# A fused decoder layer: half a weight unit copied by VectorE, gate projections copied out by ScalarE, query transposes moved

## The chip, the cores and the metric

The kernel runs on one core of one Trainium2 chip (1 of 8). The metric is the device time of one execution in microseconds (us). The core has TensorE (PE in the rows, its weight loads PEld), VectorE (DVE), ScalarE (ACT), GpSimd (POOL) and SyncE (SP, which issues the transfers). Each takes its own instructions in order.

## What is computed

One decoder layer over 512 tokens of width 1024, in float32. In the reference's words, cut:

```python
h = rmsnorm(x, g_mix)
x_rnn, g_rnn, q, k, v, gate_a, gate_b = split(h @ w_in)
y_a = (rg_lru(causal_conv(x_rnn)) * gelu(g_rnn)) @ w_rnn_proj
y_b = sliding_window_attention(q, k, v) @ w_attn_proj     # 16 query heads, 4 key heads, window 128
x = x + (sigmoid(gate_a) * y_a + sigmoid(gate_b) * y_b) @ w_out
x = x + square(relu(rmsnorm(x) @ w_up)) @ w_down
x = x + (p @ w_ple_proj) * sigmoid(rmsnorm(x) @ w_ple_gate)
```

Attention normalises queries and keys by head, rotates them, and each token sees itself and the 127 tokens ahead of it; every head has a sink value in its softmax.

## The kernel before

Activations lie transposed, features on the 128 partitions and the 512 tokens along the row. Every large product is made of three products of fp32r (a rounded float32 that TensorE takes at its full rate): a value is split into a high part, rounded to fp32r, and a low part, the rest; high x high, high x low and low x high are added up in PSUM (`mm3`, L144 to L147).

The weights come as 143 units of 128 x 1024 values. `wissue` takes the next unit of a fixed list and calls `wsplit` (L109): SyncE issues the transfer into `wr` (2 buffers), ScalarE writes the high part `wh` (L118), VectorE the low part `wl` (L119). Three further units are kept ready ahead of the one in use (`AHEAD`). The first unit comes in two halves (`parts=2`), each transferred and split on its own.

The program of PE, ACT, SP and POOL stands as the code is written; that of VectorE is put in order by a scheduler, which works from its own estimate of when operands are ready. Each engine then executes its program in that order.

The stages: at the head, `warm_up` (L207) gives TensorE `N_WARM` products of the identity, while the first chunk `x0` and the first unit arrive. For every chunk of `x`, `split_scaled` (L138, L139) writes the scaled high part of `xg` on ScalarE and the low part on VectorE. Then come keys and values (`pkv`), then queries (`pq`), L258.

The attention stage follows: eight blocks `u` = 0 to 7, each for 128 tokens (`u % 4`) and half of the heads (`u // 4`). A block works on its heads in two halves `g` = 0, 1, and between them it fills TensorE with two gate units (`pgate`, 24 matmuls each, in all 16 units: `gate_b`, then `gate_a`), whose projections need only `xg`. In TensorE's order a block is: scores of half 0 (`S`), first gate unit, transposes of the probabilities of the block before (`ppt`, half 1), scores of half 1, products with the values of the block before (`po`), half of the second gate unit (`CUT` = 4 of 8 chunks), transposes of the next block's queries (`pqt`), the other half of the unit, `ppt` of this block's half 0.

The softmax of a half runs over three engines: `softmax_max` copies the scores out (`sm`, ScalarE, L456), merges the two key blocks by `COPY_PREDICATED` (VectorE, L457), takes the maximum (`TENSOR_REDUCE`, L464), then four small operations on `st` (L465 to L468, of which L467, the negated maximum, is what the exponentials wait for). `softmax_exp` takes four exponentials and a small one on ScalarE (L474, L477). `softmax_norm` adds and inverts the sums on VectorE (L482, L483), and GpSimd multiplies (L486). `p_evac` masks the transposed probabilities into `pt` (VectorE, L505; `po` needs them). In blocks 0 and 4, whose tokens see one block of keys, VectorE reads the scores directly (L459), and `pt` is one copy on ScalarE (L503). Beside that, VectorE and ScalarE prepare queries: `q_rope` (`ra`, `rb`, L405 to L408), `q_scale` (`asq` on ScalarE, `sc` on VectorE and GpSimd, L386 to L392), the splitting of the transposed queries (`qt`, L423 and L425), and that of the attention output (`o`, L524 and L525). A gate unit leaves PSUM by `gate_evac` (L596), one multiplication on VectorE with `rb`, the reciprocal norm of the tokens.

PSUM: four tiles `mm` (`pgate`, `po` and others), two tiles `tr` (`ppt`, `pqt`), and one double tile `S` for the scores.

After attention come the recurrent branch (`px`, with the attention's projection `pyb` between), `pgl`, `pya`, the output projection, the feed-forward part (`pu`, `pd`) and the embedding part. The sigmoids of the gates are taken there by ScalarE (L750 for `gate_b`; `gate_a` ahead of `pya`).

## Time and profile before

| | |
|---|---|
| runs shown | 837.47, 838.13 and 2166.76 us; median 838.13 |
| the profiled run | 837.6 us, its span 835.5 us |
| instructions | 9915 |
| granted clock of TensorE, mean | 0.999 |
| busy | PE 829.4 us, DVE 522.1, ACT 365.0, POOL 101.4 |

The span is the profiled execution from its first to its last instruction; the 2.1 us around it belong to the run. The 2166.76 stands apart from the two others, which differ by 0.08%.

In the rows, a matmul's duration is longer than the distance to the next one, since matmuls are pipelined; distances between starts tell TensorE's speed. An instruction on VectorE may start some 0.08 us before the one ahead of it ends, if it doesn't need its result. A bracket at the end of a row gives the idle time of the engine ahead of it, and what ended it.

### The profile page before, as it was taken

To read this page: it belongs to the slowest core of one execution; us is meant where nothing else is said; L and a number is where in the kernel's file an instruction comes from. 1 tells how busy PE (TensorE), PEld (TensorE's weight loads), DVE (VectorE), ACT (ScalarE), POOL (GpSimd) and SP (SyncE) were. 2 spreads that over 40 slices of the span, in tenths; PEclk is the share of its full clock that TensorE was granted. 3 is DMA by queue.
4 is the path that set the end of the run, shared out by engine and by line. 5 is a ranking of instruction groups with operands and counts; after the bars stand their busy time and mean duration, and the time that the engine had idled before them with its cause. 6 is when DMAs were issued, how large, how long until landed. Compare 5 with 4: busy or idle time off the path is not lost.

```text
span 835.5 us, 9915 instructions
## 1 busy us (share of the span) xinstructions
PE 829.4 (99%) x3780; PEld 678.9 (81%) x3780; DVE 522.1 (62%) x768; ACT 365.0 (44%) x581; POOL 101.4 (12%) x123
## 2 busy tenths in 40 slices
PE   9999999999999999999999999999999999999997
PEld 7888877877888888888888888888888888888886
DVE  4687798886766878486567533653355435655563
ACT  7434665663578895633343221231222212333430
POOL 2922432421011110000210000000000000012100
PEclk9999999999999999999999999999999999999999
DMA  7344122122232232235333322223223232233141
GB/s 251 126 115 138 51 80 72 51 77 76 76 100 76 76 102 100 76 127 186 131 103 109 104 98 102 89 89 119 86 97 100 101 102 76 100 102 101 51 163 39
DMA packets 25744, 84.00 MB, mean 101 GB/s; under 512 B 3040, under 2 KB 3424, under 8 KB 25696
## 3 DMA queue, kind: packets, MB, share of 16 engines
q1 hardware_dynamic: 25552, 83.32, 30.0%
q8 instruction: 30, 0.49, 0.2%
q14 instruction: 18, 0.15, 0.1%
q10 hardware_dynamic: 144, 0.05, 0.0%
HBM read 80.20 MB, written 2.10 MB: 99 GB/s over the span
## 4 chain that ended last, share of the span: by engine, by line
PE 99%; DMA 0%; DVE 0%; ACT 0%; issue 0%
PE pu L145 7%; PE pd L145 7%; PE pd L147 7%; PE pu L147 7%; PE pd L146 7%; PE pu L146 7%; PE pq L258 5%; PE pgate L145 4%; PE pgate L147 4%; PE pgate L146 4%; PE pkv L258 3%; PE pyb L145 2%; PE S L441 2%; PE px L145 2%; PE pgl L145 2%; PE pyb L146 2%
## 5 line engine op out<-in xcount | busy, mean ns | idle before, releaser
L119 DVE TENSOR_TENSOR wl<-wr,wh 128x1024 fp32r<-128x1024 f32 (+1 forms) x144 | 180.6, 1257 | 56.1 <-ACT wh L118 56.1
L118 ACT ACTIVATE wh<-wr 128x1024 fp32r<-128x1024 f32 (+1 forms) x144 | 149.7, 1045 | 130.5 <-PE pd L146 98.5
L146 PE MATMUL pu<-x1g,wh 128*128 128x512 f32 x256 | 99.6, 389 | 0.0
L145 PE MATMUL pu<-x1g,wh 128*128 128x512 f32 x256 | 99.6, 389 | 0.0
L147 PE MATMUL pu<-x1g,wl 128*128 128x512 f32 x256 | 99.6, 389 | 0.0
L145 PE MATMUL pd<-u,wh 128*128 128x512 f32 x256 | 99.6, 389 | 0.0
L146 PE MATMUL pd<-u,wh 128*128 128x512 f32 x256 | 99.6, 389 | 0.0
L147 PE MATMUL pd<-u,wl 128*128 128x512 f32 x256 | 99.6, 389 | 0.0
L131 ACT ACTIVATE u<-up 128x512 fp32r<-128x512 f32 x32 | 20.2, 633 | 124.4 <-DVE up L847 124.4
L213 POOL TENSOR_TENSOR sq<-sq,sq_x 128x512 f32<-128x512 f32 x14 | 18.2, 1298 | 453.5 <-ACT sq_x L211 453.5
L856 DVE TENSOR_TENSOR xr<-pd,xr 128x512 f32<-128x512 f32 x32 | 22.1, 692 | 81.5 <-PE pd L147 81.5
L147 PEld LDWEIGHTS pu<-x1g,wl 128*128 128x128 f32 x256 | 48.0, 188 | 10.1
L147 PEld LDWEIGHTS pd<-u,wl 128*128 128x128 f32 x256 | 48.0, 188 | 10.0
L146 PEld LDWEIGHTS pd<-u,wh 128*128 128x128 f32 x256 | 48.0, 188 | 10.0
L146 PEld LDWEIGHTS pu<-x1g,wh 128*128 128x128 f32 x256 | 48.1, 188 | 10.0
L145 PEld LDWEIGHTS pd<-u,wh 128*128 128x128 f32 x256 | 48.0, 188 | 9.9
L145 PEld LDWEIGHTS pu<-x1g,wh 128*128 128x128 f32 x256 | 48.0, 188 | 9.9
L145 PE MATMUL pgate<-xg,wh 128*128 128x512 f32 x128 | 51.4, 402 | 0.0
L147 PE MATMUL pgate<-xg,wl 128*128 128x512 f32 x128 | 50.2, 392 | 0.0
L146 PE MATMUL pgate<-xg,wh 128*128 128x512 f32 x128 | 50.0, 391 | 0.0
L846 DVE TENSOR_TENSOR up<-pu,rb_x 128x512 f32<-128x512 f32 x32 | 22.0, 691 | 40.2 <-PE pu L147 40.1
L474 ACT ACTIVATE sm<-sm,st,sc 128x128 f32<-128x128 f32 x64 | 30.8, 483 | 23.6 <-DVE st L468 21.6
(225 smaller groups left out, 1620.1 us busy)
## 6 DMA issues: line engine op xcount, KB each, us to landing
wr<-in_w_all SPq DMA_DIRECT2D x142, 512.0 KB, 3.3
x<-in_x_t SPq DMA_DIRECT2D x8, 256.0 KB, 5.6
xr<-in_x_t SPq DMA_DIRECT2D x8, 256.0 KB, 3.6
out<-pgt SPq DMA_DIRECT2D x7, 256.0 KB, 2.1
kt<-kt SPq DMA_DIRECT2D x8, 128.0 KB, 2.2
wr<-in_w_all SPq DMA_DIRECT2D x2, 256.0 KB, 3.6
pk<-in_p_t SPq DMA_DIRECT2D x2, 256.0 KB, 3.8
tab<-in_ctab SPq DMA_DIRECT2D x1, 384.0 KB, 6.8
```

Of the source, the lines that this page charges most:

```text
L118: nc.scalar.activation(wh[:, c], raw[:, c], AF.Copy)
L119: nc.vector.tensor_tensor(out=wl[:, c], in0=raw[:, c], in1=wh[:, c].bitcast(F32), op=ALU.subtract)
L131: nc.scalar.activation(r[:, 0, :], src, AF.Copy)
L145: nc.tensor.matmul(out, ah, bh, start=start, stop=False)
L146: nc.tensor.matmul(out, ah, bl, start=False, stop=False)
L147: nc.tensor.matmul(out, al, bh, start=False, stop=stop)
L213: nc.gpsimd.tensor_tensor(out=acc, in0=acc, in1=t, op=ALU.add)
L258: nc.tensor.matmul(banks[n], a[:, part, n * P : (n + 1) * P], w[:, c], start=k == 0 and i == 0, stop=k == KC - 1 and i == 2)
L441: nc.tensor.matmul(pss[:, i, :], q_t[u][i % 2][:, 2 * g + i // 2, :], kt[part][:, kv, b0 * P : b0 * P + 256], start=part == 0, stop=part == 1)
L474: nc.scalar.activation(sm[:, i, :], sm[:, i, :], AF.Exp, bias=st[:, 1, i : i + 1], scale=q_sc[u][:, 4 * g + i : 4 * g + i + 1], accum_out= ...
L846: nc.vector.tensor_tensor(out=y, in0=pu, in1=r1, op=ALU.mult)
L856: nc.vector.tensor_tensor(out=x1[m], in0=pd, in1=x1[m], op=ALU.add)
```

## The change

- The first half of the first unit: its high part is written by VectorE (`tensor_copy`, `head=True`) instead of ScalarE, and issued between the high and the low part of the first `xg`; the second half stays on ScalarE. `N_WARM` is 7 instead of 8. In the first twelve products, the low part of the weights now comes second and the low part of `xg` third.
- `gate_evac` copies the gate projection out by ScalarE. The multiplication with `rb` is written where the sigmoid is taken, on VectorE, in place.
- In blocks 1 to 6 the queries' transposes stand directly behind `po`; the splitting of their result is called where the transposes stood. Their rotation (`q_rope`) stands at the start of the block.

```diff
@@ -46,7 +46,7 @@
 AHEAD = 3
 F_BUFS = 24
 W_BUFS = 4
-N_WARM = 8
+N_WARM = 7
 CUT = 4
 LAG = 2
 
@@ -102,11 +102,11 @@
     order = weight_order()
     ready = {}
 
-    def wissue(parts=1):
+    def wissue(parts=1, head=False):
         u = order.pop(0)
-        ready[u] = wsplit(u, wp, W_BUFS, parts)
-
-    def wsplit(u, pool, bufs, parts=1):
+        ready[u] = wsplit(u, wp, W_BUFS, parts, head)
+
+    def wsplit(u, pool, bufs, parts=1, head=False):
         raw = wp.tile([P, 1024], F32, tag="wr", name=f"wr{u}", bufs=2)
         wh = pool.tile([P, 1024], F32R, tag="wh", name=f"wh{u}", bufs=bufs)
         wl = pool.tile([P, 1024], F32R, tag="wl", name=f"wl{u}", bufs=bufs)
@@ -114,8 +114,11 @@
         cuts = [slice(i * n, (i + 1) * n) for i in range(parts)]
         for c in cuts:
             nc.sync.dma_start(raw[:, c], w_all[u][:, c])
-        for c in cuts:
-            nc.scalar.activation(wh[:, c], raw[:, c], AF.Copy)
+        for i, c in enumerate(cuts):
+            if head and i == 0:
+                nc.vector.tensor_copy(wh[:, c], raw[:, c])
+            else:
+                nc.scalar.activation(wh[:, c], raw[:, c], AF.Copy)
             nc.vector.tensor_tensor(out=wl[:, c], in0=raw[:, c], in1=wh[:, c].bitcast(F32),
                                     op=ALU.subtract)
         return wh, wl
@@ -133,9 +136,11 @@
             out=r[:, 1, :], in0=src, in1=r[:, 0, :].bitcast(F32), op=ALU.subtract
         )
 
-    def split_scaled(src, scale, r):
+    def split_scaled(src, scale, r, between=None):
 
         nc.scalar.activation(r[:, 0, :], src, AF.Copy, scale=scale)
+        if between:
+            between()
         nc.vector.scalar_tensor_tensor(
             out=r[:, 1, :], in0=src, scalar=scale, in1=r[:, 0, :].bitcast(F32),
             op0=ALU.mult, op1=ALU.subtract,
@@ -220,9 +225,10 @@
     for k in range(KC):
         xs.append(ftile(f"x{k}"))
         nc.sync.dma_start(xs[k], x_t[k * P : (k + 1) * P, :])
-        split_scaled(xs[k], col(V_GMIX, k), chunk(xg, k))
-        if k % 2 == 0 and k < 6:
-            wissue(2 if k == 0 else 1)
+        split_scaled(xs[k], col(V_GMIX, k), chunk(xg, k),
+                     partial(wissue, 2, True) if k == 0 else None)
+        if k in (2, 4):
+            wissue()
     for k in range(KC):
         sq_accumulate(xs[k], sqx, k == 0, f"x{k}")
     nc.sync.dma_start(rowb, row.broadcast_to([P, 144]))
@@ -252,7 +258,7 @@
                 a = chunk(xg, k)
                 todo = [(n, i) for n in range(NB) for i in range(3)]
                 if grp == k == 0:
-                    todo.sort(key=lambda v: v[1])
+                    todo.sort(key=lambda v: (0, 2, 1)[v[1]])
                 for n, i in todo:
                     part, w = ((0, wh), (1, wh), (0, wl))[i]
                     nc.tensor.matmul(banks[n], a[:, part, n * P : (n + 1) * P], w[:, c],
@@ -419,12 +425,15 @@
         qt = [att.tile([P, 4, P], F32R, tag="qt", name=f"qt{u}{j}", bufs=4) for j in range(2)]
         rows = [slice(0, HD), slice(HD, P)]
         src = [pt[own].rearrange("p (i t) -> p i t", t=P) for own in rows]
-        for j, own in enumerate(rows):
-            nc.scalar.activation(qt[j][own], src[j], AF.Copy)
-        for j, own in enumerate(rows):
-            nc.vector.tensor_tensor(out=qt[j][rows[1 - j]], in0=src[j],
-                                    in1=qt[j][own].bitcast(F32), op=ALU.subtract)
         q_t[u] = qt
+
+        def evac():
+            for j, own in enumerate(rows):
+                nc.scalar.activation(qt[j][own], src[j], AF.Copy)
+            for j, own in enumerate(rows):
+                nc.vector.tensor_tensor(out=qt[j][rows[1 - j]], in0=src[j],
+                                        in1=qt[j][own].bitcast(F32), op=ALU.subtract)
+        return evac
 
     def window(u):
         n = u % NB
@@ -582,7 +591,7 @@
     qkv_group(2, q_banks, [
         lambda: (k_transpose(norm["rot"]), q_first()),
         k_double,
-        lambda: q_transpose(0, s_banks("pqt0")[0]),
+        lambda: q_transpose(0, s_banks("pqt0")[0])(),
     ])
     rb = norm["x"]
     q_evac(1, q_banks)
@@ -593,12 +602,14 @@
 
     def gate_evac(pg, name):
         gt = ftile(name)
-        nc.vector.tensor_tensor(out=gt, in0=pg, in1=rb, op=ALU.mult)
+        nc.scalar.activation(gt, pg, AF.Copy)
         gates.append(gt)
 
     fills = [U_GB + m for m in range(KC)] + [U_GA + m for m in range(KC)]
 
     for u in range(8):
+        if 0 < u < 7:
+            q_rope(u + 1)
         w0 = wload(fills[len(gates)])
         p0 = mm_ps(f"pgate_{u}_0")
         s0 = scores(u, 0)
@@ -608,21 +619,23 @@
             p_transpose(u - 1, 1)
             p_evac(u - 1, 1)
         softmax_exp(u, 0)
-        if u < 7:
-            q_rope(u + 1)
+        if u == 0:
+            q_rope(1)
         softmax_norm(u, 0)
         if u < 6:
             q_scale(u + 2)
         gate_evac(p0, f"gate_{u}_0")
         s1 = scores(u, 1)
         if u:
-            o_split(u - 1, pv(u - 1))
+            po = pv(u - 1)
+            qt_evac = q_transpose(u + 1) if u < 7 else None
+            o_split(u - 1, po)
         softmax_max(u, 1, s1)
         w1 = ready.pop(fills[len(gates)])
         p1 = mm_ps(f"pgate_{u}_1")
         proj(p1, w1, xg, range(0, CUT))
         if u < 7:
-            q_transpose(u + 1)
+            (qt_evac if u else q_transpose(1))()
         wissue()
         softmax_exp(u, 1)
         softmax_norm(u, 1)
@@ -747,6 +760,7 @@
         if m < KC:
             x_conv(m)
         for gt in gb[m : m + 1]:
+            nc.vector.tensor_tensor(out=gt, in0=gt, in1=rb, op=ALU.mult)
             nc.scalar.activation(gt, gt, AF.Sigmoid)
         if m >= LAG:
             w = wload(U_ATT + m - LAG)
@@ -795,6 +809,7 @@
 
     mg = rtiles("mg")
     for gt in ga:
+        nc.vector.tensor_tensor(out=gt, in0=gt, in1=rb, op=ALU.mult)
         nc.scalar.activation(gt, gt, AF.Sigmoid)
     first = [(wload(U_RNN + m), mm_ps(f"pya{m}")) for m in range(2)]
     for w, py in first:
```

What becomes of the order of instructions, at three places. The first is VectorE at the head, from its first instruction on (`x_95` before and `x_94` after are the first chunk, `wr`, `wh` and `wl` the first unit). Before:

```order
L560 TENSOR_SCALAR sp<-vec 128x8
L562 TENSOR_SCALAR sp<-sp 128x8
L139 SCALAR_TENSOR_TENSOR xg_83<-x_95,vec,xg_83 128x512
L119 TENSOR_TENSOR wl_101<-wr_99,wh_100 128x512 x2
L139 SCALAR_TENSOR_TENSOR xg_83<-x_108,vec,xg_83 128x512
L139 SCALAR_TENSOR_TENSOR xg_83<-x_112,vec,xg_83 128x512
```

After:

```order
L569 TENSOR_SCALAR sp<-vec 128x8
L571 TENSOR_SCALAR sp<-sp 128x8
L144 SCALAR_TENSOR_TENSOR xg_83<-x_94,vec,xg_83 128x512
L119 CAST wh_98<-wr_97 128x512
L122 TENSOR_TENSOR wl_99<-wr_97,wh_98 128x512 x2
L144 SCALAR_TENSOR_TENSOR xg_83<-x_107,vec,xg_83 128x512
L144 SCALAR_TENSOR_TENSOR xg_83<-x_111,vec,xg_83 128x512
```

The copy (`CAST`) stands behind the low part of the first `xg`, and the two low parts of the unit behind the copy.

The second place is VectorE at the start of block 2: `sm` from `S` is the first half's scores, `pt` the masked probabilities of block 1's second half. Before, from `COPY_PREDICATED` to the sum (L482):

```order
L457 COPY_PREDICATED sm_1044<-tab,S_1035 128x512
L464 TENSOR_REDUCE st_1047<-sm_1044 128x4
L465 TENSOR_TENSOR st_1047<-st_1047,sc_775 128x4
L466 TENSOR_TENSOR st_1047<-st_1047,rowb 128x4
L467 TENSOR_SCALAR st_1047<-st_1047 128x4
L468 TENSOR_TENSOR st_1047<-rowb,st_1047 128x4
L505 TENSOR_TENSOR pt_1082<-ppt_1077,tab 128x512
L505 TENSOR_TENSOR pt_1084<-ppt_1077,tab 128x512
L405 TENSOR_TENSOR ra_1091<-q_518,cc_q 128x512
L406 TENSOR_TENSOR rb_1092<-q_518,ss_q 128x8x32
L407 TENSOR_TENSOR rb_1092<-q_518,ss_q 128x8x32
L482 TENSOR_TENSOR st_1047<-st_1047 128x4
```

After, from the `wl` ahead of it to the sum (L491):

```order
L122 TENSOR_TENSOR wl_1035<-wr_1033,wh_1034 128x1024
L414 TENSOR_TENSOR ra_1027<-ra_1027,rb_1028 128x512
L466 COPY_PREDICATED sm_1049<-tab,S_1040 128x512
L514 TENSOR_TENSOR pt_1087<-ppt_1082,tab 128x512
L473 TENSOR_REDUCE st_1052<-sm_1049 128x4
L514 TENSOR_TENSOR pt_1089<-ppt_1082,tab 128x512
L474 TENSOR_TENSOR st_1052<-st_1052,sc_774 128x4
L763 TENSOR_TENSOR gate_1_1016<-gate_1_1016,rb_x 128x512
L475 TENSOR_TENSOR st_1052<-st_1052,rowb 128x4
L476 TENSOR_SCALAR st_1052<-st_1052 128x4
L477 TENSOR_TENSOR st_1052<-rowb,st_1052 128x4
L491 TENSOR_TENSOR st_1052<-st_1052 128x4
```

`ra` and `rb` have moved from behind the `pt` to ahead of `COPY_PREDICATED`; the maximum stands between the two `pt`, the multiplication of a gate (L763, now from and to SBUF) between the maximum and the negation; the sum follows the small operations with nothing between.

The third place is ScalarE in the same block, from the exponentials of the first half on. Before:

```order
L474 ACTIVATE sm_1044,st_1047<-sm_1044,st_1047,sc_775 128x128 x4
L477 ACTIVATE st_1047<-st_1047 128x4
L386 ACTIVATE asq_1103<-q_698 128x512
L524 ACTIVATE o_706<-po_1120 128x4x128
L456 ACTIVATE sm_1127<-S_1111 128x512
L423 ACTIVATE qt_1154<-pqt_1149 64x512
L423 ACTIVATE qt_1155<-pqt_1149 64x512
L118 ACTIVATE wh_1161<-wr_1160 128x1024
L474 ACTIVATE sm_1127,st_1130<-sm_1127,st_1130,sc_775 128x128 x4
L477 ACTIVATE st_1130<-st_1130 128x4
L118 ACTIVATE wh_1201<-wr_1200 128x1024
L456 ACTIVATE sm_1216<-S_1207 128x512
```

After:

```order
L483 ACTIVATE sm_1049,st_1052<-sm_1049,st_1052,sc_774 128x128 x4
L486 ACTIVATE st_1052<-st_1052 128x4
L392 ACTIVATE asq_1102<-q_697 128x512
L605 ACTIVATE gate_0_1108<-pgate_0_1039 128x512
L533 ACTIVATE o_705<-po_1119 128x4x128
L465 ACTIVATE sm_1133<-S_1110 128x512
L432 ACTIVATE qt_1129<-pqt_1124 64x512
L432 ACTIVATE qt_1130<-pqt_1124 64x512
L121 ACTIVATE wh_1160<-wr_1159 128x1024
L483 ACTIVATE sm_1133,st_1136<-sm_1133,st_1136,sc_774 128x128 x4
L486 ACTIVATE st_1136<-st_1136 128x4
L605 ACTIVATE gate_1_1188<-pgate_1_1142 128x512
```

Two copies of gates have come in: one ahead of `o` and of the second half's scores, one behind the second half's exponentials and ahead of the next unit's `wh`.

## Rows read from the trace of the kernel before

**Rows 1.** The page, busy time, share of the span and instructions by engine.

```profile
PE 829.4 (99%) x3780; PEld 678.9 (81%) x3780; DVE 522.1 (62%) x768; ACT 365.0 (44%) x581; POOL 101.4 (12%) x123
```

**Rows 2.** Timeline of TensorE at the head: start and duration in us, engine, line, operation.

```profile
1.34 3.59 PE L207 MATMUL pw<-ident 128*128 128x128 f32 x16 [1.34 <-POOL ident masks.py:199]
5.21 2.11 PE L258 MATMUL pkv<-wh,xg 128*128 128x512 f32 x8 [0.28 <-ACT wh L118]
```

**Rows 3.** Stretches from second scores on: length, busy PE, PEld, DVE, ACT, POOL; clock, DMA.

```profile
109.51:126.03 16.52, 16.52 (x85) 12.99 (x86) 15.33 (x38) 9.80 (x27) 5.25 (x9) 1.00 0.24 84
126.03:142.24 16.21, 16.21 (x87) 12.61 (x86) 14.67 (x33) 9.04 (x26) 5.25 (x9) 1.00 0.20 65
...
173.87:190.72 16.85, 16.85 (x88) 12.91 (x86) 14.86 (x36) 9.60 (x28) 3.86 (x8) 1.00 0.29 91
190.72:203.15 12.43, 12.43 (x62) 9.26 (x61) 9.46 (x23) 6.63 (x20) 1.41 (x4) 1.00 0.15 48
```

**Rows 4.** Timeline of VectorE in block 2 and at the start of block 3.

```profile
108.10 0.74 DVE L457 COPY_PREDICATED sm<-tab,S 128x512 f32<-128x512 int32 x1
...
109.79 0.16 DVE L466 TENSOR_TENSOR st<-st,rowb 128x4 f32<-128x4 f32 x1
109.98 0.17 DVE L467 TENSOR_SCALAR st<-st 128x4 f32<-128x4 f32 x1
...
111.33 0.68 DVE L405 TENSOR_TENSOR ra<-q,cc_q 128x512 f32<-128x512 f32 x1
111.93 0.42 DVE L406 TENSOR_TENSOR rb<-q,ss_q 128x256 f32<-128x256 f32 x1
...
122.53 1.23 DVE L119 TENSOR_TENSOR wl<-wr,wh 128x1024 fp32r<-128x1024 f32 x1
123.67 0.73 DVE L457 COPY_PREDICATED sm<-tab,S 128x512 f32<-128x512 int32 x1
```

**Rows 5.** Timeline of ScalarE at the head, the first half unit's high part.

```profile
4.55 0.61 ACT L118 ACTIVATE wh<-wr 128x512 fp32r<-128x512 f32 x1
```

**Rows 6.** Timeline of VectorE at the head, the low parts of `xg` and of the first half unit.

```profile
4.68 0.75 DVE L139 SCALAR_TENSOR_TENSOR xg<-x,vec,xg 128x512 fp32r<-128x512 f32 x1 [0.37 <-ACT xg L138]
5.34 0.69 DVE L119 TENSOR_TENSOR wl<-wr,wh 128x512 fp32r<-128x512 f32 x1
```

**Rows 7.** VectorE by line and shape, first 80 us: busy us, mean ns, idle before.

```profile
L309 DVE COPY kv<-pkv 128x512 f32<-128x512 f32 x2 | 1.3, 676 | 0.0
...
L198 DVE TENSOR_SCALAR nt_x<-nt_x 128x512 f32<-128x512 f32 x1 | 0.4, 416 | 0.0
```

**Rows 8.** Stretches of TensorE: a split gate unit, its transposes, an unsplit unit; columns as above.

```profile
128.99:135.06 6.07, 6.07 (x30) 4.96 (x29) 5.26 (x12) 3.33 (x5) 3.02 (x5) 1.00 0.00 0
131.85:132.20 0.35, 0.35 (x5) 0.35 (x4) 0.34 (x1) 0.00 (x0) 0.35 (x1) 1.00 0.00 0
193.67:199.26 5.59, 5.59 (x27) 4.57 (x26) 3.63 (x8) 3.08 (x8) 1.06 (x4) 1.00 0.12 26
```

**Rows 9.** Timeline of ScalarE in block 2, from the first half's exponentials.

```profile
110.25 0.49 ACT L474 ACTIVATE sm<-sm,st,sc 128x128 f32<-128x128 f32 x1 [2.70 <-DVE st L468]
...
112.17 0.19 ACT L477 ACTIVATE st<-st 128x4 f32<-128x4 f32 x1
112.27 0.61 ACT L386 ACTIVATE asq<-q 128x512 f32<-128x512 f32 x1
112.84 0.60 ACT L524 ACTIVATE o<-po 128x512 fp32r<-128x512 f32 x1
```

**Rows 10.** Timeline of GpSimd, two normalisations of a half (four operations each).

```profile
106.91 2.46 POOL L486 TENSOR_SCALAR sm<-sm,st 128x128 f32<-128x128 f32 x4 [5.57 <-ACT wh L118]
114.48 1.41 POOL L486 TENSOR_SCALAR sm<-sm,st 128x128 f32<-128x128 f32 x4 [5.11 <-DVE sc L390]
```

**Rows 11.** Stretches at the end, columns as in rows 3; the granted clock is third from last.

```profile
831.00:832.00 1.00, 0.06 (x1) 0.00 (x0) 0.93 (x4) 0.00 (x0) 0.00 (x0) 1.00 0.00 0
834.20:835.40 1.20, 0.00 (x0) 0.00 (x0) 0.00 (x0) 0.00 (x0) 0.00 (x0) 0.50 0.00 0
```

## The prediction, made before the changed kernel ran

> **What bounds the kernel now.** I read the page's busy shares first, then the rows in which TensorE stands idle, then stretches of the attention stage engine by engine. TensorE is busy for 829.4 us, 99% of the span [rows 1], and its only idle times ahead of an instruction are 1.34 us at the start and 0.28 us before the first product, which waits for the first `wh` [rows 2]. So a gain can come only from that wait, from switching between kinds of matmul, or from fewer matmuls; a loss from anything that makes TensorE wait. In attention the cover is thin. An ordinary block (one `u`, two gate units) takes TensorE 16.21 us, and VectorE is busy for 14.67 of them [rows 3]. VectorE and ScalarE work in order, and each half of a block is a chain: scores, `COPY_PREDICATED`, maximum, exponentials on ScalarE, sum and reciprocal on VectorE, normalisation on GpSimd, transposes `ppt`, masked copies `pt`, products `po`. Before, one turn of VectorE, from the first `COPY_PREDICATED` of block 2 to that of block 3, takes 123.67 - 108.10 = 15.57 us [rows 4], 0.6 less than TensorE's block. The scores have one PSUM tile (`bufs=1`), so the second scores of a block cannot start before the first `COPY_PREDICATED` has read it.
>
> **The head.** Now `wh` is on ScalarE from 4.55 for 0.61 us, to 5.16 [rows 5], and the first product starts at 5.21 [rows 2]. The copy on VectorE was to run beside ScalarE's `xg`. But VectorE's order shows the low part of `xg` first and the copy behind it; that low part needs ScalarE's `xg` and starts at 4.68, and what follows it starts at 5.34 [rows 6]. So the copy starts at 5.34. The trace has no copy from SBUF to fp32r. Bounds: 0.42 us (one source, SBUF to SBUF) and 0.68 us (a copy out of PSUM) [rows 7]; I take 0.42, since source and target are in SBUF. With 0.05 us from the end of `wh` to the product, the first product starts at 5.81, **0.60 us later** (0.86 at the other end). The Trainium skill ("VectorE: DVE Perf Modes", section on the fixed extra latency of SBUF sources) gives an fp32 copy inside SBUF 58 + 512/2 cycles at 0.96 GHz, 0.33 us, as an estimate; by it the term were 0.51.
>
> What follows is in time: `wl` of the first half runs behind the copy, from 5.8 for 0.69 us [rows 6], and is wanted 0.9 us (four products) after 5.81; the low part of `xg` is now ready before it is wanted, and ScalarE, which has lost a copy, is not later than before. So the stream shifts by 0.60. One warm-up matmul less (2 of 16 records) saves nothing: the warm-up ends at 4.93 [rows 2], about 4.5 then, ahead of the wait either way.
>
> **Attention, saved on TensorE.** The queries' transposes split a gate unit: first half, transposes and second half take 6.07 us; the transposes 0.35 of it; an unsplit unit behind `po` takes 5.59 [rows 8]. With the transposes behind `po`, a block saves up to 6.07 - 5.59 - 0.35 = **0.13 us**, 0.8 in six blocks; nothing, if `po` to `pqt` costs what `pgate` to `pqt` did.
>
> **Attention, VectorE and ScalarE.** VectorE keeps as many operations: a gate's multiplication, still some 0.68 us for 512 elements (`ra`, inside SBUF [rows 4]), only reads SBUF instead of PSUM. ScalarE gets 16 copies out of PSUM of 0.60 each (the row of `o<-po` [rows 9]). What matters is VectorE's order. The `ra` and `rb` of the next queries used to run while ScalarE took the first half's exponentials; now they stand behind the second half's reciprocal, ahead of the next `COPY_PREDICATED`. The first half's maximum now stands between the two `pt`, a gate multiplication between the maximum and the exponentials, and the sum directly behind the exponentials, with nothing ahead of it.
>
> I walk an ordinary block by start distances of [rows 4]: 0.60 from one 512-element operation to the next if it doesn't need it (0.08 less than its duration, so 0.66 behind `COPY_PREDICATED`), 0.08 between small ones, 0.20 where one needs the other, 1.15 behind `wl`. Zero is the first `COPY_PREDICATED`.
> - `pt` 0.66, maximum 1.26, `pt` 1.86, small 2.46, gate 2.54, small 3.14, negation 3.34 to 3.51, exponentials from 3.53. Before: 110.25 - 108.10 = 2.15 [rows 4, 9].
> - The exponentials and the small one behind them end 2.11 after their start (110.25 to 112.36 [rows 9]), so the sum comes at 5.68. ScalarE goes on with the square 5.55 to 6.16, gate 6.12, `o` 6.69, copied scores 7.2 to 7.8; VectorE with `sc` 6.2, gate 6.8, `o` 7.5, second `COPY_PREDICATED` 8.1.
> - `qt` 8.76, maximum 9.36, `qt` 9.96, small 10.56, `wl` 10.63, small 11.78, negation 11.98. Exponentials 12.18 to 14.29; VectorE meanwhile has one `pt` only.
> - Sum 14.33, `pt` 14.41, reciprocal 15.0, `ra` 15.1, `rb` 15.7 and 16.0, `wl` 16.4 (its `wh` stands behind the gate copy on ScalarE), `ra` 17.5, next `COPY_PREDICATED` **18.1**.
>
> So a turn goes from 15.6 to 18.1 us against TensorE's 16.1: VectorE's order becomes the bound, by 2.0 us a block. About 3.6 us of a turn are idle, the exponentials of both halves without cover.
>
> **Where TensorE then stands.** I carry this through the blocks and give the lag of the second scores (without the head); the starts before are the bounds of the stretches in [rows 3].
> - Block 2: transposes come 2.8 us earlier and with them block 1's second exponentials, 0.45 earlier; but two `rb`, two `ra` and `wl` ahead put the first `COPY_PREDICATED` at 109.35 instead of 108.10. Scores 110.1 for 109.51: **+0.6**.
> - Block 3: 109.35 + 18.1 + 0.8 = 128.25 for 126.03: **+2.2**.
> - Block 4 attends to one block only; its maximum reads PSUM without ScalarE's copy, so the scores are free, but `ppt` waits for the normalisation: reciprocal at 15.5 of the turn, 1.4 on GpSimd [rows 10]. Scores 144.85 for 142.24: **+2.6**. Then `po` waits 0.7 for `pt`.
> - Block 5 has one `pt` a half, on ScalarE, and slack: **+3.1**. Block 6 runs the ordinary turn behind it: `COPY_PREDICATED` at 177.05, scores 177.85 for 173.87, **+4.0**, of which 0.6 come back, since TensorE now loses them there anyway (16.85 us for that block against 16.21).
> - Block 7: 194.15 for 190.72, **+3.4**. The last `ppt` waits for the last normalisation on VectorE: 207.95 for 203.15, **+4.8**.
>
> Behind that, weights are three units ahead and no engine is late. **Sum:** 0.6 + 4.8 = 5.4 us, TensorE's 0.13 a block included. The profiled run took 837.6 us, 835.5 of them the span; the median of the runs shown, 838.13, is 0.06% above it. Forecast 837.6 + 5.4 = **843.0 us**, 0.6% slower.
>
> Bounds: head 0.5 to 0.9. Attention: lower end 3, if ScalarE's copies overlap enough to make a turn 17.6; upper end 9, if the normalisation's first step is held up as in 2.46 against 1.41 us [rows 10], 1.05 in each of four blocks whose `ppt` waits for it.
>
> **Rivals.**
> 1. *VectorE's turn does not bind* (not slower). If the pieces overlap so that a turn stays below 16.2, the change does what it says: 0.6 lost at the head, 0.8 saved in switches, up to 0.95 in the short waits of blocks 2 and 6 (16.52 and 16.85 against 16.21 [rows 3]): 836.4, or 838.2 with none of it saved. It decides if 1.9 of my 18.1 us are wrong. For it: before, a turn stayed under 16.2. Against: the uncovered exponentials follow from the order and the rows alone. Chance 0.14.
> 2. *GpSimd holds `ppt` up too*, the upper end: 847 us. For it, two of its rows differ by 1.05 us; against, the long one met a busy VectorE. Chance 0.07.
> 3. *The clock falls* (slower by over 2%). At the end the granted clock reads 1.00 while TensorE is already idle, and 0.50 later in the same idle stretch [rows 11]: 1.2 instead of 2.4 GHz. My waits are 0.5 to 1.6 us each, 1.3 at the head. If one grew to the idle stretch of the end, the 48 gate products of a block, 5.59/24 = 0.23 us each [rows 8], would cost 11.2 us more at half clock: 854 for one such block, 865 for two. The Trainium skill ("TensorE: Matmul & The Clock Gate", "Why this matters for your kernels") warns of long idle gaps between bursts for this reason; the trace's last rows agree. Against: no wait that I work out comes near that stretch. Chance 0.04.
> 4. *The forecast*, 2 to 8 us slower in all: 0.75; its own range is 840 to 846.
>
> **How the numbers follow.** The range 837.5 to 848 holds the forecast, rival 2 and the upper part of rival 1. Faster by over 2% (16.8 us, about what a measurement of this kernel can tell from no change) is more than any gain there is, 0.01; slower by as much needs rival 3, 0.03; within 2% 0.96.
>
> **What would show it.** First `pkv` at 5.8 us, right behind VectorE's copy; second scores waiting for `COPY_PREDICATED`; VectorE's idle time ended by ScalarE's `st` in each half; turns of 18 us in blocks 2, 3 and 6; the last `ppt` near 208.6. It is wrong if TensorE shows no wait on VectorE between 108 and 208 us, if turns stay under 16.2, or if the first product starts before 5.2.

## The result, and the profile after the change

The changed kernel takes 852.01 us in the median of four runs (851.89 to 854.5); runs of the kernel before beside them have a median of 838.06. The ratio, worked out from the single runs and not from the two medians, is 1.0175, with a 95% interval of 1.0163 to 1.0187. By the medians the kernel is 14.0 us slower, where 5.4 were forecast, and outside the range of 837.5 to 848. Single runs that stand far apart from the others of their kernel (2166.76 us of the kernel before, 1195.15 of e2 and 2982.54 of g3 below) are left out of ratios and intervals, and as the last two were the profiled ones, no rows of e2 and g3 are read. The profiled run is the slowest of the four, 854.5 us, with a span of 852.4, so 16.9 more than the span of 835.5 before. All rows below are from it.

The page: busy time, share of the span and instructions by engine.

```profile
PE 836.6 (98%) x3778; PEld 681.1 (80%) x3778; DVE 523.7 (61%) x769; ACT 371.4 (44%) x596; POOL 112.6 (13%) x123
```

Against [rows 1], ScalarE has its 15 copies more, VectorE is almost the same, and GpSimd, whose instructions nobody touched, is busy for 11.2 us more with the same 123 instructions. That number points to a cause that the prediction had priced far too low.

What TensorE waits for between 70 and 225 us: engine, operation, line, released by; us in total, times, longest.

```profile
PE ppt L503 <- POOL sm L495: 6.0, 8, 1.3
PE S L450 <- DVE qt L434: 1.5, 2, 0.8
PE ppt L503 <- DVE sm L495: 0.8, 1, 0.8
```

Before, TensorE had no such row there. The prediction's wait (second scores behind `COPY_PREDICATED`) is not among them; the transposes `ppt` ahead of the scores wait for GpSimd first. The two waits for `qt` stand in the first scores of blocks 3 and 4, for which the queries' low parts come late.

The stretches from second scores to second scores, as in [rows 3] (length, busy PE, PEld, DVE, ACT, POOL; clock, DMA):

```profile
114.21:133.65 19.44, 17.27 (x85) 12.86 (x86) 15.03 (x33) 10.36 (x28) 7.01 (x9) 1.00 0.14 51
133.65:153.70 20.05, 17.54 (x85) 12.86 (x86) 16.05 (x38) 12.88 (x38) 7.01 (x9) 1.00 0.16 54
188.46:206.21 17.75, 17.19 (x86) 12.87 (x86) 12.80 (x28) 9.84 (x27) 4.57 (x8) 1.00 0.17 58
```

They were 16.52, 16.21 and 16.85 long. VectorE has about as much to do as before over the three; GpSimd has 7.01 instead of 5.25 in the first two.

VectorE and GpSimd at the end of the turn that leads to block 2, where block 1's second half is normalised:

```profile
109.98 0.17 DVE L492 RECIPROCAL st<-st 128x4 f32<-128x4 f32 x1
110.06 0.66 DVE L411 TENSOR_TENSOR ra<-q,cc_q 128x512 f32<-128x512 f32 x1
110.64 0.42 DVE L412 TENSOR_TENSOR rb<-q,ss_q 128x256 f32<-128x256 f32 x1
110.97 0.42 DVE L413 TENSOR_TENSOR rb<-q,ss_q 128x256 f32<-128x256 f32 x1
111.31 1.31 DVE L122 TENSOR_TENSOR wl<-wr,wh 128x1024 fp32r<-128x1024 f32 x1
112.54 0.68 DVE L414 TENSOR_TENSOR ra<-ra,rb 128x512 f32<-128x512 f32 x1
113.14 0.72 DVE L466 COPY_PREDICATED sm<-tab,S 128x512 f32<-128x512 int32 x1
```

```profile
110.68 0.86 POOL L495 TENSOR_SCALAR sm<-sm,st 128x128 f32<-128x128 f32 x1 [6.64 <-DVE st L492]
111.53 1.85 POOL L495 TENSOR_SCALAR sm<-sm,st 128x128 f32<-128x128 f32 x1
113.36 0.37 POOL L495 TENSOR_SCALAR sm<-sm,st 128x128 f32<-128x128 f32 x1
```

A step of GpSimd takes 0.37 us alone. Here the first ends 0.15 us after the second `rb`, the second 0.16 us after the last `ra`: each ends only when VectorE is through with a run of operations that read two operands from SBUF, and the third takes 0.37 us under `COPY_PREDICATED`, which reads PSUM. That VectorE's operands are the reason is tested below (f4). The four steps take 3.39 us instead of 1.41 [rows 10]. TensorE there:

```profile
111.89 0.27 PE L503 MATMUL ppt<-ident,sm 128*128 128x128 f32 x1
113.43 1.02 PE L503 MATMUL ppt<-ident,sm 128*128 128x128 f32 x3 [1.26 <-POOL sm L495]
114.21 1.19 PE L450 MATMUL S<-kt,qt 128*128 128x256 f32 x8
```

The head, TensorE and VectorE, as in [rows 2] and [rows 6]:

```profile
1.34 3.36 PE L212 MATMUL pw<-ident 128*128 128x128 f32 x14 [1.34 <-POOL ident masks.py:199]
6.19 2.04 PE L264 MATMUL pkv<-wh,xg 128*128 128x512 f32 x4 [1.49 <-DVE wh L119]
8.03 1.91 PE L264 MATMUL pkv<-wl,xg 128*128 128x512 f32 x4
```

```profile
4.96 0.75 DVE L144 SCALAR_TENSOR_TENSOR xg<-x,vec,xg 128x512 fp32r<-128x512 f32 x1 [0.37 <-ACT xg L141]
5.62 0.42 DVE L119 CAST wh<-wr 128x512 fp32r<-128x512 f32 x1
```

The copy stands behind the low part of `xg`, as the order said, and takes 0.42 us. But then four products take 2.04 us, where before eight took 2.11 [rows 2], and the next four 1.91. Attention starts 3.1 us late. The packed trace lists the granted clock as entries, and the first, full speed, stands at 10.74 us here and at 4.61 us in the kernel before, in both where TensorE's distances halve; the clock column reads 1.00 ahead of it only because nothing is listed there. So the slow products ran at half clock (1.2 GHz).

Last, the granted clock around the wait in block 4 (columns as above, clock third from last):

```profile
150.92:154.00 3.08, 1.38 (x6) 0.81 (x7) 2.07 (x4) 2.56 (x10) 2.63 (x3) 1.00 0.23 57
154.00:158.00 4.00, 4.00 (x16) 1.89 (x14) 2.73 (x7) 0.00 (x0) 1.82 (x5) 0.57 0.22 87
158.00:159.00 1.00, 1.00 (x8) 0.69 (x6) 0.00 (x0) 0.58 (x1) 1.00 (x1) 1.00 0.00 0
```

After 2.79 us in which the four `ppt` crept along behind GpSimd, TensorE worked at half clock (1.2 GHz) for most of the next four: a mean of 0.57 is 3.4 us at 0.5. The scores took 1.64 us for 1.11, `po` 2.93 for 1.87, together 1.6 us more.

So the profiled run's 16.8 us up to the last `ppt` are 3.1 at the head, 1.6 for the clock in block 4 and 12.1 for the rest of attention. The other three runs are 2.4 to 2.6 us shorter, and no profile shows where.

### The profile page after: what moved, and what is told of

It reads as the page before. It is cut to its first block, busy times and chain, and to the rows that moved or that the text cites. A ratio compares the mean times of both kernels' runs of the same rounds, so it can differ in the third digit from the quotient of the medians.

```text
span 852.4 us, 9930 instructions
## 1 busy us (share of the span) xinstructions
PE 836.6 (98%) x3778; PEld 681.1 (80%) x3778; DVE 523.7 (61%) x769; ACT 371.4 (44%) x596; POOL 112.6 (13%) x123
## 4 chain that ended last, share of the span: by engine, by line
PE 87%; DVE 6%; ACT 3%; POOL 2%; issue 1%; DMA 0%; POOLq 0%; ACTq 0%
PE pu L150 7%; PE pd L152 7%; PE pu L152 7%; PE pd L150 7%; PE pd L151 7%; PE pu L151 7%; PE pq L264 5%; PE pkv L264 3%; ACT sm L483 2%; PE pyb L150 2%; PE pgl L150 2%; PE ppg L151 2%; PE ppg L152 2%; PE pgl L151 2%; PE pout L151 2%; PE pout L150 2%
## 5 line engine op out<-in xcount | busy, mean ns | idle before, releaser
L495 POOL TENSOR_SCALAR sm<-sm,st 128x128 f32<-128x128 f32 x60 | 39.3, 672 | 93.9 <-DVE st L492 45.7
```

What stands on the lines that cost most here:

```text
L495: eng.tensor_scalar(out=sm[:, i, :], in0=sm[:, i, :], scalar1=den[:, i : i + 1], scalar2=1.0, op0=ALU.mult, op1=ALU.mult)
```

## The experiments

Where times are compared, the kernel before ran beside them; its median was between 837.78 and 838.17.

### The two parts apart, and the warm-up

`e1` is the kernel before with the head's edits alone, `e2` the same with more warm-up, `e3` the change without the head's edits:

```diff
-N_WARM = 7
+N_WARM = 10
```

> The head part alone (copy on VectorE, 7 warm-up products, the new order of the first twelve products); attention as before. Theory H1 (the longer idle time makes TensorE run its first products at half its rate): first product at 5.8 to 6.2 us, the first ten or so 0.43 us apart instead of 0.23, first query product some 2.5 to 3.2 us later than before: 840.3 to 841.0 us. Theory H0 (only the later copy, as predicted): 838.2 us, products 0.23 us apart.

> The head part alone with 10 warm-up products instead of 7, so that they end at about 5.8 us and TensorE does not stand idle ahead of the first product. H1: the products 0.23 us apart from the first on, first product at 5.9 to 6.3, 838.3 to 838.8 us, so about 2 us less than with 7. If the slow products come from the copy or the new order and not from the idle time: as with 7 (840.3 to 841.0).

> The attention part alone (gates on ScalarE, transposes behind the products with the values), head as before. With H1 the loss splits into 2.5 to 3.2 us of the head and the rest here: 848.5 to 849.5 us. With H0 nearly all is here: 851.3. In either case the transposes of the probabilities of the second half wait for GpSimd, 1.2 to 2.5 us in each of blocks 2, 3, 4, 6 and 7.

Measured: e1 839.59 us (837.68 to 840.31), 1.75 slower than before (ratio 1.0014, 1.0004 to 1.0023); e2 838.41, 0.57 slower (1.0005, 0.9995 to 1.0015); e3 850.95, 13.1 slower (1.016, 1.0145 to 1.0175). The head of e1:

```profile
5.73 2.04 PE L264 MATMUL pkv<-wh,xg 128*128 128x512 f32 x4 [1.03 <-DVE wh L119]
...
9.28 1.76 PE L264 MATMUL pkv<-wh,xg 128*128 128x512 f32 x6
```

Nine products are some 0.43 us apart, then it is 0.23, and the first entry of full clock stands there (9.74). e1's ten runs fall in two groups, four of 837.7 to 838.2 and six of 839.5 to 840.3. The profiled run is of the second, with the slow products; that the first group is without them is not shown, but likely. With ten warm-up products nine runs lie between 837.8 and 838.6, so none is in the second group. e1's first product starts 0.52 us later than before (5.73 for 5.21), near the 0.60 that the prediction gave the later copy; e2's 0.57 agrees, but is not clear of zero. The slow products cost the rest, some 1.2 us. The distances in e1's profiled run are those of H1, but its median lies between H0's 838.2 and H1's 840.3 to 841.0, and e3's 850.95 is nearer to H0's 851.3: H1 holds in some runs, not in every one.

How long TensorE stays slow differs between executions of heads that are alike, too. In e3, whose head is that of before, the first five products were 0.43 apart (clock entry at 7.39), in the profile of before none. Whether the missing warm-up product or the longer idle time keeps it slow is open, since e2 changed both. A missing product is not needed: in f4 below, with all eight and an idle time of 0.64 us, nine products were slow (entry at 9.51). Nor does such an idle time always do it: in h1 it was 0.57 us, the clock had risen within the warm-up (4.23), and no product was slow.

### GpSimd held up by VectorE: a probe

In the kernel before, one operation of VectorE is added behind the reciprocal of a first half; its result goes nowhere:

```diff
+        if g == 0 and 0 < u < 7:
+            if u % 3 == 1:
+                stt(out=dmy, in0=tab[:, 0:512], scalar=sc1, in1=tab[:, 256:768], ...)
+            elif u % 3 == 2:
+                stt(out=dmy, in0=p0, scalar=sc1, in1=tab[:, 256:768], ...)
+            else:
+                nc.vector.tensor_scalar(out=dmy, in0=tab[:, 0:512], scalar1=sc1, ...)
```

> The kernel before with one more operation of 128x512 on VectorE behind the reciprocal of the first half, while GpSimd normalises: in blocks 1 and 4 with two operands from SBUF, in blocks 2 and 5 the same operation with one operand from PSUM and one from SBUF, in blocks 3 and 6 a multiplication by a column, with one operand from SBUF. T1: the GpSimd step that meets it takes 0.7 to 1.1 us instead of 0.37 in blocks 1 and 4 and ends shortly behind the VectorE operation; 0.37 in blocks 2 and 5. If any busy VectorE slowed GpSimd: long steps in all six. If nothing does: 0.37 in all six.

Measured in one run (850.22 us, with the added work). The added operations, by line (two from SBUF; PSUM and SBUF; one from SBUF): durations min/median/max in ns, first and last start.

```profile
L490 DVE SCALAR_TENSOR_TENSOR dmy<-tab,st x2: 742/748/753, 100.9 to 154.1; 128x512 f32<-128x512 f32 x2
L493 DVE SCALAR_TENSOR_TENSOR dmy<-pgate,st,tab x2: 752/752/752, 118.2 to 171.3; 128x512 f32<-128x512 f32 x2
L496 DVE TENSOR_SCALAR dmy<-tab,st x2: 480/483/486, 138.7 to 190.4; 128x512 f32<-128x512 f32 x2
```

The GpSimd step that met the first of each:

```profile
100.92 1.00 POOL L500 TENSOR_SCALAR sm<-sm,st 128x128 f32<-128x128 f32 x1
118.35 0.38 POOL L500 TENSOR_SCALAR sm<-sm,st 128x128 f32<-128x128 f32 x1 [5.35 <-ACT asq L386]
138.73 0.73 POOL L500 TENSOR_SCALAR sm<-sm,st 128x128 f32<-128x128 f32 x1
```

Two operations of the same length, 0.75 us: the one with both operands in SBUF stretches the step to 1.00 us (0.86 in block 4), the one with an operand in PSUM leaves it at 0.38. The multiplication by a column, with one operand, all in SBUF, stretches it as well (0.73 and 0.57), which the expectation had left open. The Trainium skill ("SBUF — State Buffer", section "Who interferes with whom") states this: VectorE and GpSimd share a pair of SBUF ports, and VectorE contends for it with a GpSimd instruction that reads SBUF when it has two SBUF inputs itself, or in its two-port modes. The trace agrees (1.00 and 0.73 us against 0.38). It was a rule that spoke against this change, and the prediction did not use it.

### What GpSimd costs in the change

`e4` gives the second halves' normalisation to ScalarE, `f3` leaves it out:

```diff
+            if g == 1 and u < 7:                       # e4
+                nc.scalar.activation(sm[:, i, :], sm[:, i, :], AF.Copy, scale=den[:, i : i + 1])
+                continue
```

```diff
-        for i in range(4):                             # f3
+        for i in range(0 if g == 1 and u < 7 else 4):
```

> The attention part alone, with the normalisation of the second halves on ScalarE (four scaled copies) instead of GpSimd; VectorE's order stays that of the attention part. Theory T1 (GpSimd's normalisation stands still while VectorE reads two operands from SBUF): no wait of the transposes for GpSimd, turns of VectorE of about 18 us instead of 17.4 to 20.2, the loss falls to the 4.8 us of the prediction's walk or a little above: 842 to 844.5 us. Theory T2 (VectorE's order alone makes the turn, GpSimd's wait only shows it): turns stay at 19 to 20 us and the time within 1.5 us of the attention part alone (848 to 850).

> The attention part alone, without GpSimd's normalisation of the second halves of blocks 0 to 6 (left out; the order of VectorE and ScalarE is unchanged). T1: TensorE waits for the scores' tile instead (the predicated copy, as predicted), turns of 18 to 19 us, 843 to 845.5 us, so about half of the loss is GpSimd's. T2: turns and time as in the attention part alone, 849 to 851 us.

Measured: e4 854.05 us, slower than the attention part alone and against both theories. TensorE's longest wait there:

```profile
PE S L444 <- DVE sm L460: 10.1, 5, 2.9
```

The waits for GpSimd are gone, but ScalarE waits for the reciprocal and then copies for 1.2 us ahead of the gate and the next `wh`; VectorE's `wl` comes later, and a turn is 132.27 - 112.27 = 20.0 us long. Behind two of these waits, 2.91 and 2.10 us long, the granted clock fell to a half for 3.4 us each (means of 0.57 from 114 to 118 us and 0.51 from 206.7 to 210.2). One wait took the place of another: e4 decides nothing on GpSimd. f3 does, with no other engine loaded: 844.89 us, 6.1 below e3. TensorE's longest wait and the first `COPY_PREDICATED` of blocks 2 and 3:

```profile
PE S L444 <- DVE sm L460: 4.3, 4, 1.5
```

```profile
110.63 0.72 DVE L460 COPY_PREDICATED sm<-tab,S 128x512 f32<-128x512 int32 x1
...
129.27 0.72 DVE L460 COPY_PREDICATED sm<-tab,S 128x512 f32<-128x512 int32 x1
```

Now TensorE waits where the prediction put it, and a turn is 18.64 us. The 6.1 us are an upper bound for what VectorE's hold on GpSimd costs, since the undisturbed 1.41 us of normalisation are left out with it.

### Gates and transposes apart

`f1` has only the gates of the change, `f2` only the transposes and the rotation.

> Of the whole change only the gates: copied out by ScalarE, multiplied with the norm on VectorE from SBUF; transposes and rotation where they were. By the order, the gate's multiplication and the next unit's low part stand behind the reciprocal of the second half, the rotation still in the first half. Theory T1 (GpSimd's normalisation stands still while VectorE reads two operands from SBUF): the normalisation of the second half takes 2.5 to 3.5 us and the transposes wait for it, turns of about 18.5 us, 844 to 846 us. Theory T2 (only VectorE's order counts): turns of about 17.2, 840 to 842 us.

> Of the whole change only the transposes behind the products with the values and the rotation at the start of a block; gates as before on VectorE. The rotation runs here under the exponentials of the second half, its last addition and the low part of the next unit behind the reciprocal. T1: the normalisation takes 2.5 us or more, 840 to 843 us. T2: turns of 16.6, 838.5 to 840 us.

Measured: f1 849.45 us, 11.5 slower (1.0136, 1.0119 to 1.0153); f2 839.64, 1.65 slower (1.0021, 1.0012 to 1.003). Together 13.1, as in e3. f2 lies in the range of T2; for f1 both theories were too low. VectorE there:

```profile
107.47 0.17 DVE L483 RECIPROCAL st<-st 128x4 f32<-128x4 f32 x1
107.55 0.66 DVE L750 TENSOR_TENSOR gate<-gate,rb_x 128x512 f32<-128x512 f32 x1
108.36 1.26 DVE L119 TENSOR_TENSOR wl<-wr,wh 128x1024 fp32r<-128x1024 f32 x1
109.55 0.72 DVE L457 COPY_PREDICATED sm<-tab,S 128x512 f32<-128x512 int32 x1
...
117.39 0.69 DVE L750 TENSOR_TENSOR gate<-gate,rb_x 128x512 f32<-128x512 f32 x1
```

The turn is 18.76 us (109.55 to 128.31) though the rotation has not moved. A gate's copy stands on ScalarE behind the exponentials, so its multiplication cannot run under them; it comes behind the reciprocal, where it pushes back `wl`, `o` and `COPY_PREDICATED`, and holds GpSimd.

### Is it the place of the operations, or ScalarE's copies?

`h1` is f1 with each gate's multiplication issued behind the next half's negated maximum, under its exponentials:

```diff
+        with tc.issue_after(negs[u, g]):     # negs: the instruction of L467
+            scale_gates()                    # gate *= rb, of the gates copied out so far
```

> Gates copied out by ScalarE as in the change, transposes and head as before, but each gate's multiplication is issued on VectorE directly behind the negated maximum of the next half, so under ScalarE's exponentials and not behind a reciprocal. Theory T3 (the gates cost 11.5 us because their multiplication went from under the exponentials to behind them, where it stands ahead of the predicated copy and holds GpSimd's normalisation): turns of 16 to 17 us, the normalisation of the second half at 2.5 us or less, 838 to 842 us. Theory T4 (ScalarE's sixteen copies out of PSUM cost, by coming ahead of the scores' copy and of the high parts of the weights): 846 us or more.

Measured: 840.37 us, 2.2 slower than before (1.0027, 1.0016 to 1.0039), 9.1 below f1. T3 holds: with the same copies on ScalarE, four fifths of the loss go with the place of one operation on VectorE.

`g1` keeps the early transposes, but rotates a block ahead, in the old place under the first half's exponentials; `g2` pins the head's copy ahead of the low part of `xg`, with 8 warm-up products; `g3` has both:

```diff
-            q_rope(u + 1)                    # under the first half's exponentials
+            q_rope(u + 2)
```

> Transposes directly behind the products with the values, as in the change, but the rotation is done one block earlier, in its old place under the first half's exponentials, so nothing is added behind the reciprocal; gates on VectorE and head as before. If the loss of the transposes-only kernel came from the rotation behind the reciprocal (GpSimd held up, transposes waiting 0.5 to 1.2 us in blocks 2, 3, 4 and 6): those waits are gone, a block keeps the 0.1 us saved, 837.2 to 837.8 us. If the early transposes themselves cost: 839 to 840.

> The head part with the copy pinned ahead of the low part of the first xg in VectorE's order, and 8 warm-up products; attention as before. First product at 4.9 to 5.0 us instead of 5.21, right behind the warm-up, products 0.23 us apart: 837.5 to 837.8 us, and runs closer together than with the head part as it is (837.7 to 840.3). If the first half unit's transfer lands too late for it: as before or up to 838.4.

> Both together: rotation a block ahead, transposes behind the products with the values, copy pinned first with 8 warm-up products, gates on VectorE. The two gains add up: 836.8 to 837.5 us, 0.5 to 1.2 below before. If either fails: 837.8 or more.

Measured: g1 839.91 us (1.0021, 1.0012 to 1.0031), g2 837.83 (1.0001, 0.9992 to 1.001), g3 839.68 (1.002, 1.0011 to 1.0029). The gains that were expected of g1 and g3 are not there, and the rotation was not the cause of f2's loss. The head's pin gains nothing clear of noise: g2's first product came at 5.17 us, where 4.9 to 5.0 was expected. VectorE in block 2 of g1, from the second `COPY_PREDICATED` to the negated maximum:

```profile
116.28 0.73 DVE L460 COPY_PREDICATED sm<-tab,S 128x512 f32<-128x512 int32 x1
117.04 0.69 DVE L428 TENSOR_TENSOR qt<-pqt,qt 64x512 fp32r<-64x512 f32 x1
117.76 0.69 DVE L467 TENSOR_REDUCE st<-sm 128x4 f32<-128x512 f32 x1
...
119.28 1.22 DVE L119 TENSOR_TENSOR wl<-wr,wh 128x1024 fp32r<-128x1024 f32 x1
...
121.21 0.16 DVE L470 TENSOR_SCALAR st<-st 128x4 f32<-128x4 f32 x1
```

The negation, for which the exponentials wait, comes 4.93 us behind the copy; in f2 it is 4.94 (116.67 to 121.61), in the kernel before 3.65 (115.51 to 119.16). Because the transposes are done earlier, the scheduler takes `qt` ahead of the maximum and `wl` and a gate ahead of the negation. So `h2` pins what is not urgent behind the negation; `h3` is h2 with g2's head, and `i1` has the change's parts together, gates on ScalarE included, pinned like this; its rotation is a block ahead, its gates' multiplications stand as in h1, and it has 8 warm-up products:

```diff
+            with tc.issue_after(negs[u, 0]):
                 p_evac(u - 1, 1)
...
+        with tc.issue_after(recs[u, 0]):     # recs: the reciprocal, L483
             gate_evac(p0, f"gate_{u}_0")
...
+        with tc.issue_after(negs[u, 1]):     # queries' low parts, wl, second gate
```

> The kernel with the rotation a block ahead and transposes behind the products with the values (839.9 us), with VectorE's order pinned: the negated maximum of a half ahead of the masked copies, of the queries' low parts and of the unit's low part. If those, which the scheduler took ahead because the transposes come earlier, made the loss of 1.8 us: second half's negation back at 3.0 to 3.7 us behind its predicated copy instead of 4.9, waits of the transposes for GpSimd in at most block 6, 837.0 to 838.0 us. If the loss lies elsewhere: 839 to 840.

> The same with the copy of the first half unit pinned first and 8 warm-up products. If both gains hold: 836.5 to 837.6 us, 0.4 to 1.5 below before; 838 or more if the order was not the cause.

> All of the change's edits, with VectorE's order pinned as in the best version (negation ahead of masked copies, queries' and units' low parts; rotation a block ahead; gates' multiplications behind the next half's negation; first copy pinned, 8 warm-up products). If the whole loss of the change came from VectorE's order: 836.0 to 837.0 us, as the best version. If ScalarE's sixteen gate copies cost by themselves (they stand ahead of the scores' copy and of the high parts): 838 to 841 us, with waits of TensorE for the scores' copy or for pt.

Measured: h2 836.52 us (0.9979, 0.997 to 0.9988); h3 836.37 (0.9976, 0.9967 to 0.9985); i1 837.27 (0.9993, 0.9984 to 1.0002). h3 is 1.8 us faster than the kernel before and 15.6 faster than the change. In h2, stretches from second scores to second scores, and VectorE in block 2:

```profile
109.04:125.16 16.12, 16.12 (x88) 12.60 (x86) 14.80 (x33) 10.04 (x29) 5.40 (x9) 1.00 0.22 75
125.16:141.28 16.12, 16.12 (x88) 12.60 (x86) 14.76 (x33) 8.97 (x26) 5.40 (x9) 1.00 0.19 67
172.66:188.78 16.12, 16.12 (x88) 12.60 (x86) 12.55 (x27) 10.58 (x32) 2.82 (x8) 1.00 0.23 78
```

```profile
114.46 0.73 DVE L460 COPY_PREDICATED sm<-tab,S 128x512 f32<-128x512 int32 x1
115.23 0.69 DVE L467 TENSOR_REDUCE st<-sm 128x4 f32<-128x512 f32 x1
...
116.34 0.17 DVE L470 TENSOR_SCALAR st<-st 128x4 f32<-128x4 f32 x1
```

The negation comes 1.88 us behind the copy. These blocks take 16.12 us each, against 16.52, 16.21 and 16.85 before, and between the warm-up and 225 us TensorE waits for no one. GpSimd's second normalisation still takes 2.38 us in block 2, under `wl`, but now early enough to be covered. How much of h2's gain is the early transposes' and how much the pins' is not separated: the kernel before with the pins alone was not run.

i1, between its two expectations, does not differ clearly from the kernel before, though ScalarE copies the gates out and the transposes come early. So the loss in attention lay in VectorE's order, and nearly none of it in ScalarE's copies or the early transposes as such. The gates' part is not quite free: i1 is 0.9 us above h3, which differs from it in the gates alone (1.3, if each is taken against the runs of the kernel before beside it). The head's edits add nothing clear: h3 and h2 differ by 0.15 us.

## Why the prediction was wrong

The side was right, the size was not. The prediction took 2% for about what a measurement of this kernel can tell from no change; the interval above is 0.24% wide. The lag of the second scores against before, in us, each kernel's own delay at the start of attention taken off (starts read from TensorE's timeline):

| | forecast | change | e3, attention alone | f3, no second normalisation |
|---|---|---|---|---|
| block 2 | 0.6 | 1.6 | 1.6 | 1.1 |
| block 3 | 2.2 | 4.5 | 4.5 | 3.2 |
| block 4 | 2.6 | 8.4 | 8.4 | 3.9 |
| block 5 | 3.1 | 9.8 | 8.2 | 4.9 |
| block 6 | 4.0 | 11.5 | 9.9 | 6.3 |
| block 7 | 3.4 | 12.4 | 10.8 | 6.2 |
| last `ppt` | 4.8 | 13.7 | 12.3 | 6.9 |

- **The step that failed: "reciprocal at 15.5 of the turn, 1.4 on GpSimd."** The normalisations that start at 110.68, 129.95 and 149.99 us took 3.39, 3.56 and 3.55 us. The forecast's upper end let one step be held by 1.05 us, as the long row of [rows 10] showed, and called the reason "a busy VectorE". The reason was in the rows of the kernel before: the first step of that row lies under a `wl`, with both operands in SBUF (VectorE, kernel before).

```profile
106.95 1.23 DVE L119 TENSOR_TENSOR wl<-wr,wh 128x1024 fp32r<-128x1024 f32 x1 [0.57 <-ACT wh L118]
```

  The walk itself listed what comes behind the reciprocal now, `ra`, `rb`, `rb`, `wl`, `ra`, all of that kind and 3.1 us long, and did not put the two together. That is rival 2, given 0.07, with a larger price. The cost: 1.07 us of a turn (19.71 against 18.64), and in block 4, where `ppt` takes the whole delay, 3.8 us where 0.4 was forecast; f3 shows 0.65 there. Up to the last `ppt` it is 5.4 us (12.3 in e3 against 6.9 in f3). These are upper bounds, since f3 lacks the undisturbed 1.41 us as well. The reciprocal was late, too: it stood 16.8 us into the turn that leads to block 4 (132.85 to 149.63), where the prediction had 15.5, and 15.0 in its own walk.
- **The turn.** 18.1 us was forecast, 18.64 measured without GpSimd's second normalisation, so the walk by start distances was 0.5 short. That and `po` in block 4 (in f3 1.26 us late where 0.7 was forecast) are the larger parts of the remaining 6.9 against 4.8. In the change itself the turn was 132.85 - 113.14 = 19.71.
- **Order as the bound.** Right: VectorE's idle times are ended by ScalarE's `st` (2.18 and 1.46 us in block 2 of the change), because nothing is left to run under the exponentials. With the gates' multiplications put back there, most of f1's loss is gone (h1); with the rest pinned behind the negation as well, nothing clear is left of the change's (i1).

```profile
119.57 0.16 DVE L491 TENSOR_TENSOR st<-st 128x4 f32<-128x4 f32 x1 [2.18 <-ACT st L486]
128.90 0.16 DVE L491 TENSOR_TENSOR st<-st 128x4 f32<-128x4 f32 x1 [1.46 <-ACT st L486]
```

- **The wait.** Second scores were to wait for `COPY_PREDICATED`. In the change `ppt` ahead of them waits for GpSimd, and the scores start 0.35 us after that copy has ended (113.86 against 114.21), so this wait hides the other; f3 uncovers it.
- **The head.** 0.60 for the later copy was near (0.52 in e1's trace). "One warm-up matmul less (2 of 16 records) saves nothing" counted only what it saves. That TensorE may run its first products at half clock had no term in the sum: some ten of them in the profiled run, 1.2 us in the median of e1. Whether the missing product helped to bring it about is open.
- **Transposes.** A block saves 0.10 us, with 0.13 at most forecast: `pqt` 0.41 and an unsplit unit 5.56 make 5.97 in the change against 6.07 [rows 8]. That part of the change is good, and h2, where TensorE does not wait, keeps it (0.41 and 5.55).
- **The clock.** Rival 3's mechanism appeared in the profiled run at a small price, 1.6 us. In e3 the same wait of 2.79 us in block 4 left the clock at 1.00, so it does not follow every time. The mean granted clock of the change's four runs is 0.995 to 0.997, that of e3's 0.998 to 0.999, so the clock seems to have fallen in each of them.

## What to carry to other kernels

Where one engine's order is made by a scheduler and the rest is written by hand, the price of moving an operation is the order that comes out: look up what now stands between the operation on the critical chain and its inputs, and pin the chain's head ahead of the fillers. An operation that can run under a wait is nearly free there; moved behind it, it can cost most of its length: f1 and h1 differ by 9.1 us, 0.57 for each of sixteen multiplications of some 0.68 us. Before placing VectorE work beside GpSimd work, see where its operands lie.

## What the runs showed of the hardware

- A GpSimd step that reads SBUF is held while VectorE runs an operation with two operands in SBUF, and also during a plain multiplication by a column with one: 1.00 and 0.73 us for a step of 0.37, ending 0.15 to 0.30 us after VectorE's operation. With one of two operands in PSUM it is not (0.38).
- At the head TensorE may run its first products 0.43 us apart instead of 0.23, for none to ten of them, and it differs between executions. The trace's first clock entry, full speed, stands where the distances halve (4.61 us in the kernel before, 7.39 in e3, 9.74 in e1, 10.74 in the change). The Trainium skill ("TensorE: Matmul & The Clock Gate", "Part 1: The HAM clock gate") gives 0.427 us for such a product at 1.2 GHz, and the distance agrees.
- The warm-up itself runs at the slow rate for the most part: in g2 its records are 0.21 us apart up to 4.06 us and 0.11 from 4.25 on, with the first clock entry at 4.20.
